# Who adds the residual, the weight sums and one low part: VectorE or transfers that accumulate, in the projection of a two-layer encoder trunk

## The chip, the core and the metric

The kernel runs on one core of a Trainium2 chip. A core has TensorE (PE, matrix products into PSUM), VectorE (DVE), ScalarE (ACT), GpSimd (POOL) and SyncE (SP), each of which runs its own list of instructions in order, and DMA engines that move data between HBM and the on-chip memory SBUF. Here SP issues nearly all loads and stores. POOL issues transfers that accumulate: they add what they carry to what lies at the destination. The metric is the device time of one launch in microseconds (us), the median of the runs.

## The reference

Two requests of 512 and 256 tokens (768 together) of width 1024 pass through two layers, all in fp32: layer 0 mixes tokens by windowed attention, layer 1 by a gated short convolution; each is followed by a squared-ReLU MLP of width 4096 and a gated input embedding.

```python
def short_conv(h, w_in, conv_w, w_out):
    b_gate, c_gate, u = jnp.split(h @ w_in, 3, axis=-1)
    z = c_gate * u
    ...                                   # conv: width 3 over tokens
    return (b_gate * conv) @ w_out

def trunk(x, p, ...):
    for i in range(DEPTH):                # 2
        h = rms_norm(x, norm_mix[i])
        x = x + (window_attention(h, ...) if i % 2 == 0 else short_conv(h, ...))
        h = rms_norm(x, norm_mlp[i])
        x = x + jnp.square(jax.nn.relu(h @ mlp_w_up[i])) @ mlp_w_down[i]
        gate = jax.nn.sigmoid(rms_norm(x, norm_ple[i]) @ ple_w_gate[i])
        x = x + (p[i] @ ple_w_proj[i]) * gate
    return rms_norm(x, final_norm)
```

The place of the change is the last line of `short_conv` in layer 1: the product with `w_out` (1024 x 1024), its addition to the residual `x`, and the start of the MLP behind it.

## The kernel before

**Stages.** By the trace, attention takes 0 to 285 us, the MLP of layer 0 to about 700, its gate and embedding to about 820, the product with `w_in` and the convolution to 1000 (12 chunks), the projection with `w_out` 1000 to 1067 (4 chunks), the MLP of layer 1 to about 1470, and the last gate, embedding and norm the rest.

**Products.** Activations lie with their features on the 128 partitions and tokens along the free axis, `x(0)` to `x(7)` being 128 x 768 tiles. A product of two blocks of weights with two blocks of activations is made with seven products in place of eight (a Strassen scheme; H = 384 is half of the tokens). Each needs a sum or difference of weight blocks (class `Weights7`) and of activation blocks. To keep fp32 accuracy, every operand is split: a high part, ACT's copy into the fp32r type (`whi`, `vhi`, `zhi`, line 922), and a low part, DVE's subtraction `src - hi` (`wlo`, `vlo`, `zlo`, line 933). PE computes high x high, high x low and low x high: 8 + 4 matmuls of 128 x 384 for each of the seven products (line 954). In some chunks, chunk 0 of the projection and the first of the MLP among them, a few are done apart with a smaller depth (line 966, `closing` and `parts`, whose operands stand at lines 866 to 879).

**A chunk** (`seven_parts`) handles a pair of weight tiles `r1`, `r2` (`wraw`, 128 x 1024, three places in SBUF). Its operands are four groups: `direct` (`whi`, `wlo`, from `r1`), `w22` (`vhi`, `vlo`, from half of `r2`), `s32` (`zhi`, `zlo`, from the sum tile `a`) and `s14` (`whi`, `wlo`, from the sum tile `b`). The sum tiles are called `sum`. They are made for the next chunk while the present one runs, on DVE: `sums32` makes `a` (lines 893, 894), `sums14` makes `b` (lines 901, 903), four operations of 128 x 512 in all. `zhi` and `zlo` have one place each, `whi` and `wlo` two. The order of the seven products on PE is `yh,whi`, then `t,zhi` into `b`, `t,zhi` into `a`, `yh,whi` into `c`, `t,whi` into `a`, `t,vhi` into `d`, `yh,whi` into `a`; each high half is followed by its low half. Behind the first product ACT copies `a` into `c` (line 2039), behind the second `b` into `p` (2046), behind the third `a` into `d` (2051); the products that follow need the copied places.

**Sums by transfers.** For the pairs named in `GATHERED` the sums are not made on DVE but by `gathered`: SP loads four halves of 256 KB into `a` and `b` (line 845), and POOL issues four accumulating transfers (line 847): 512 KB, 256, 256 and, from `a` into `b` within SBUF, 256 KB. In the projection these are chunk 1 and pair 4, which is the first chunk of the MLP (`first_up`). (Two more pairs elsewhere are gathered too; they stay.)

**The residual.** Before the projection, `x` has been stored into HBM as `xp` (line 2349). `Joined(c)` takes the products of chunk c into `x(c)` and `x(c + 4)`. For chunks in `BY_DMA` (0 and 1) it writes the product alone, two of the four quarters by ACT copies (lines 2763 and 2776), two by DVE (2755 and 2770), and afterwards POOL adds `xp` by two accumulating transfers of 384 KB (line 2936). For chunks 2 and 3 SP loads `xp` back into `x` first (line 2928) and DVE adds (lines 2758, 2759, 2765, 2772 and 2778). When `x(m)` is complete, `nxt.block` squares it for the next norm (`sq`, line 637) and `nxt.combine` makes the MLP's operands from it (`q`, `t`, `xs`).

**The order.** All of this is written once into a `Recorder`, which notes each operation with a cost in us and a delay until its result is there (`Recorder.add`), sets up a list schedule from them, and then issues the five engines' instructions in that order. So a cost or an operation that changes can move other operations too. The instructions of one engine stay in the order chosen, whatever really arrives first.

Of the kernel before, what the change touches and what calls it, by code (L numbers as in the profile page):

```python
# [17 lines left out]
AF = mybir.ActivationFunctionType  # L18
ALU = mybir.AluOpType
# [6 lines left out]
KB = D // P  # L26
# [7 lines left out]
CH = 1024  # L34
# [13 lines left out]
H = T // 2  # L48
# [68 lines left out]
def size(x):  # L117
    n = 1
    for m in x.shape[1:]:
        n *= m  # L120
    return n
# [26 lines left out]
class Recorder:  # L148
# [85 lines left out]
    def add(self, engine, what, run, outs, ins, line, table=None):  # L234
        n = max([1] + [size(ap) for ap in outs])
        if engine == "PE":
            cost = {384: 0.1735, 256: 0.121, 512: 0.23, 128: 0.11}.get(n, n * 0.45e-3)
            lag = cost + 0.16
        elif engine == "DVE":
            cost = 0.07 + n * 1.042e-3 + 0.06 * (what == "scalar_tensor_tensor" and n > 384)  # L240
            lag = cost + 0.082
        elif engine == "ACT" and what == "dma_start":
            cost, lag = 0.1, 4.0
        elif engine == "ACT":
            cost = 0.032 + n * 0.911e-3 + 0.09 * (len(ins) > 1)
            lag = cost + 0.095
            if table is not None:
                if table != self.tables[0]:
                    cost += 1.3
                    lag += 1.3  # L250
        elif engine == "SP":
            cost, lag = 0.46, 4 * P * n / 350e3
        elif what == "dma_start":
            cost, lag = 3.5, 5.0
        else:
            cost, lag = 0.3, 0.4
        op = Recorded(engine, run, cost, lag, line)
        op.size, op.due = n, self.due
        for ap in ins:
            self.touch(op, ap, False)  # L260
        for ap in outs:
            self.touch(op, ap, True)
        if self.also is not None:
            op.pre[self.also] = True
        if table is not None:
            if self.tables[1] is not None:
                op.pre.setdefault(self.tables[1], False)
            self.tables = table, op
        self.ops.append(op)
        return op  # L270
# [187 lines left out]
def trunk_kernel(ctx: ExitStack, tc: tile.TileContext, a: dict, out: bass.AP):  # L458
    nc = tc.nc
    record = Recorder(tc)  # L460
    act, dve, pe, sp, pool = (
        record.engine(*z)
        for z in ((nc.scalar, "ACT"), (nc.vector, "DVE"), (nc.tensor, "PE"), (nc.sync, "SP"), (nc.gpsimd, "POOL"))
    )
# [38 lines left out]
    def home(source, n, dt, tag, name, bufs=1):  # L503

        def make():
            return source.tile([P, n], dt, tag=tag, name=name, bufs=bufs)

        return make() if record.closed else record.new(tag, bufs, make, [P, n], dt)

    def fetch(src):  # L510
        raw = home(wp, CH, F32, "wraw", "wraw", 3)
        sp.dma_start(raw[:, : src.shape[1]], src)
        return raw
# [92 lines left out]
    class Norm:  # L606


        n = T

        def __init__(self, i, name, places, acc, rstd=None):
            self.i, self.name, self.places, self.rplace = i, name, places, rstd
            self.xs = [None] * KB, [None] * KB
            self.aplace, self.begun = acc, False
# [159 lines left out]
    class Sums:  # L774
# [20 lines left out]
        def high(self, i):  # L795
            t = [slot(self.places[2 * i + p], "t7") for p in range(2)]
            act.activation(t[0][:], (self.q1, self.q2)[i][:], AF.Copy)  # L797
            self.keep(t, (("t1", "t3"), ("t4", "t2"))[i])
            self.t = self.t + [t] if i else [t]
# [38 lines left out]
    def sum_places():  # L838
        return [home(more, CH, F32, f"sum{i}", "sum") for i in range(2)]

    def gathered(src1, src2):
        half, other = slice(0, 512), slice(512, CH)
        a, b = sum_places()
        for t, c, src in ((a, half, src1[:, half]), (a, other, src1[:, half]), (b, half, src2[:, half]), (b, other, src1[:, other])):
            sp.dma_start(t[:, c], src)
        for to, src in ((a[:], src2), (a[:, other], src2[:, half]), (b[:, half], src2[:, other]), (b[:, other], a[:, other])):
            pool.dma_start(to, src, accum_op=ALU.add)
        return a, b

    class Weights7:  # L850

        def __init__(self, src1, src2, sums=None):
            self.moved = sums is not None
            self.raw = [fetch(src1), fetch(src2)]
            self.w, self.parts, self.due, self.apart = {}, {}, set(), None
            self.s = sums or sum_places()
# [36 lines left out]

        def sums14(self, part=None):
            if self.moved:
                return
            (r1, r2), (a, b) = self.raw, self.s
            if part != 1:  # L900
                dve.tensor_tensor(b[:, :512], r2[:, :512], r2[:, 512:], ALU.add)
            if part != 0:
                dve.tensor_tensor(b[:, 512:], r1[:, 512:], a[:, 512:], ALU.add)

        def high(self, group):

            self.due.add(group)
            names = self.GROUPS[group]
            if group in ("s32", "s14"):
                src = self.s[group == "s14"][:]  # L910
            else:
                src = self.raw[group != "direct"][:, CH - 512 * len(names) :]
            n = len(names) * 512
            if group == "s32":
                tag = "z"
            else:
                tag = "v" if group == "w22" else None
            if tag is None:
                hi, lo = (home(wp, CH, F32R, f"w{p}", f"w{p}", 2) for p in ("hi", "lo"))
            else:  # L920
                hi, lo = (home(more, n, F32R, f"{tag}{p}", f"{tag}{p}") for p in ("hi", "lo"))
            act.activation(hi[:], src, AF.Copy)  # L922
            self.parts[group] = hi, lo, src
            for i, k in enumerate(names):
                c = slice(512 * i, 512 * i + 512)
                self.w[k] = hi[:, c], lo[:, c]
# [284 lines left out]
    def mixer_attention():  # L1211
# [109 lines left out]
        def split_op(hi, lo, src, n, ready, keys):  # L1321

            def high():
                act.activation(hi.t[:, :n], src()[:, :n], AF.Copy)

            def low():
                dve.tensor_tensor(lo.t[:, :n], src()[:, :n], hi.t[:, :n].bitcast(F32), ALU.subtract)

            h = first(hi, "ACT", A(n), high, ready, keys)
            return h, first(lo, "DVE", V(n), low, [h], [*keys, hi.key])  # L1330
# [597 lines left out]

    PAIRED = [m + i for m in range(KB // 2) for i in (0, KB // 2)]

    def up_chunk(l, u):
        f = 4 * (u // 2) + u % 2
        return Weights7(a["up"][l, f], a["up"][l, f + 2])


    def run(steps, n=None):
# [146 lines left out]
    def mlp(l, norm, nxt, w, places, early, spare, product=None, follow=None, closing=None):  # L2083
# [207 lines left out]
        with record.as_written({ET.Activation, ET.PE, ET.DVE}):  # L2291
            if product:
                ahead(norm, product, w, places[3:5] + places[6:7] + places[12:])
            for i, (job, *args) in enumerate(jobs):

                def make():

                    if i + 1 == len(jobs):
                        return None
                    what, *n = jobs[i + 1]  # L2300
                    if what is not down:
                        return up_chunk(l, *n)
                    k = (KB // 2) * n[0] + 2 * n[1]
                    return Weights7(a_down[k], a_down[k + 1])

                a_down = a["down"][l]
                w = job(*args, w, make, None)
            assert not pend
            return w
# [467 lines left out]
            else:  # L2777
                dve.tensor_tensor(self.one[:, H:], self.one[:, H:], a, ALU.add)

    GATHERED, BY_DMA = (1, 4), (0, 1)  # L2780

    def mixer_conv(norm, w, early, nxt, wide, held, yplaces, parts, closing=None, closing_out=None):

# [55 lines left out]
        class Out:  # L2839
            def __init__(self, kind):  # L2840
                self.kind = kind
# [38 lines left out]

        def out_weights(c):
            f = a["w_out"][c], a["w_out"][c + KB // 2]
            return Weights7(*f, sums=gathered(*f) if c in GATHERED else None)

        def first_up():
            f = a["up"][1, 0], a["up"][1, 2]
            return Weights7(*f, sums=gathered(*f) if KB // 2 in GATHERED else None)

        with record.as_written({ET.Activation, ET.PE, ET.DVE}):
            for n in range(3 * KB // 2):  # L2890
                j, kind = divmod(n, 3)
                bs = []
                last = n == 3 * KB // 2 - 1
# [58 lines left out]
    for i, m in enumerate(PAIRED):  # L2952
        if i == 1:
            w += [weight(a["w_o0"][3], 4)] * 2
        ps = both()
        if m < KB // 2:
            group2(ps, terms_of(w[m], [p[4:] for p in aos], col=m % 2 * P))
        else:
            group2(ps, terms_of(w2, [p[6:] for p in aos], col=(m - 4) * P))
        add(m, ps, xa[m])  # L2960
        n1.block(m, x(m))
        behind(i)
# [121 lines left out]
```

## Time and profile before

| what | us |
| --- | --- |
| median of 3 runs (1617.63, 1617.76, 1621.16) | 1617.76 |
| the profiled execution | 1618.11 |
| its span on the core | 1616.3 |
| PE busy, of the span | 1600.6 (99%) |
| DVE busy | 1410.8 (87%) |
| ACT busy | 978.9 (61%) |
| POOL busy (transfers it issues) | 117.4 (7%) |
| mean granted clock of PE | 0.997 |

The busy time of an engine counts its instructions, not the waits between them; the granted clock is the share of full speed that the chip let PE run at. In timelines a row is a start, a duration, the engine, the line of the kernel, output and inputs, and in brackets the time for which the engine was idle before it with what ended that idle time. `a<-t,zhi` means that `a` is written from `t` and `zhi`. The durations of neighbouring instructions overlap a little, as engines are pipelined. The 1.8 us between the span and the device time lie outside the core's instructions.

### The profile page before, as it was taken

The numbers are of one execution on the slowest core, as the hardware profiler recorded it, in microseconds if no ns is written. First come the engines' busy times: TensorE is split into PE (matmuls) and PEld (weight loads), VectorE is DVE, ScalarE is ACT, GpSimd is POOL, SyncE is SP. The second block draws the span as 40 slices with busy tenths as digits, with TensorE's granted clock in tenths as the row PEclk, the third lists the DMA queues.
The fourth block names the chain that finished last, engine by engine and source line by source line (L and its number), as shares of the span: only waits on it lengthen the run. The fifth ranks groups of instructions, "written<-read, shape, count | busy, mean of one in ns | idle before, by whom it ended". The sixth has DMA issues, their size and how long they took to land.

```text
span 1616.3 us, 24519 instructions
## 1 busy us (share of the span) xinstructions
PE 1600.6 (99%) x9217; PEld 1551.9 (96%) x9217; DVE 1410.8 (87%) x2300; ACT 978.9 (61%) x1574; POOL 117.4 (7%) x178
## 2 busy tenths in 40 slices
PE   9999999999999999999999999999999999999998
PEld 7988889999999999999999999899999999999987
DVE  7579997998888888999899988799988988889986
ACT  7378887765555555556684435576555545546655
POOL 1001000010110110100000000100110011010000
PEclk9999999999999999999999999999999999999999
DMA  8745314243433343315432213642443343342232
GB/s 298 214 122 150 111 37 131 105 114 83 117 108 93 100 104 94 103 66 153 139 107 91 73 71 86 182 111 78 119 105 93 103 114 87 87 118 78 85 122 88
DMA packets 68563, 179.45 MB, mean 111 GB/s; under 512 B 8379, under 2 KB 24123, under 8 KB 68444
## 3 DMA queue, kind: packets, MB, share of 16 engines
q1 hardware_dynamic: 51596, 152.06, 27.9%
q0 software_dynamic: 16704, 25.70, 9.8%
q8 instruction: 72, 1.18, 0.3%
q14 instruction: 47, 0.39, 0.1%
q10 hardware_dynamic: 144, 0.13, 0.0%
HBM read 135.39 MB, written 13.11 MB: 92 GB/s over the span
## 4 chain that ended last, share of the span: by engine, by line
PE 93%; ACT 3%; DVE 2%; DMA 1%; issue 1%; SPq 0%; POOL 0%; DVEq 0%; ACTq 0%; POOLq 0%
PE a L954 40%; PE b L954 10%; PE mm L436 8%; PE c L954 6%; PE d L954 6%; PE gate L558 4%; PE B L954 4%; PE C L954 4%; PE gate L2409 3%; PE O L436 2%; PE S L436 2%; PE pt L436 2%; PE vp L436 1%; PE mm L558 1%; DMA sum<-sum 0%
## 5 line engine op out<-in xcount | busy, mean ns | idle before, releaser
L933 DVE TENSOR_TENSOR zlo<-sum,zhi 128x1024 fp32r<-128x1024 f32 x80 | 97.7, 1221 | 61.1 <-ACT zhi L922 61.0
L922 ACT ACTIVATE whi<-sum 128x1024 fp32r<-128x1024 f32 x80 | 84.9, 1062 | 96.2 <-PE a L954 82.9
L922 ACT ACTIVATE vhi<-wraw 128x512 fp32r<-128x512 f32 x80 | 50.5, 631 | 140.9 <-PE B L954 62.5
L954 PE MATMUL a<-xs,whi 128*128 128x384 f32 x692 | 134.6, 334 | 0.0
L2241 POOL DMA_DIRECT2D x<-p x96 | 83.9, 874 | 681.5 <-issue 396.1
L954 PE MATMUL a<-t,zhi 128*128 128x384 f32 x610 | 126.9, 337 | 3.6 <-ACT c L2039 3.6
L954 PEld LDWEIGHTS a<-xs,whi 128*128 128x128 f32 x692 | 121.2, 188 | 0.2
L954 PE MATMUL a<-t,whi 128*128 128x384 f32 x562 | 116.1, 335 | 0.5 <-ACT d L2051 0.5
L954 PE MATMUL b<-t,zhi 128*128 128x384 f32 x562 | 116.3, 334 | 0.0
L954 PEld LDWEIGHTS a<-t,zhi 128*128 128x128 f32 x610 | 108.4, 189 | 4.5 <-ACT c L2039 4.5
L922 ACT ACTIVATE zhi<-sum 128x1024 fp32r<-128x1024 f32 x80 | 84.7, 1059 | 42.4 <-PE a L954 31.9
L954 PE MATMUL a<-act,whi 128*128 128x384 f32 x512 | 109.3, 334 | 0.0
L933 DVE TENSOR_TENSOR wlo<-sum,whi 128x1024 fp32r<-128x1024 f32 x80 | 97.4, 1218 | 5.0 <-ACT whi L922 5.0
L954 PEld LDWEIGHTS a<-t,whi 128*128 128x128 f32 x562 | 99.0, 188 | 1.4 <-ACT d L2051 1.3
L954 PEld LDWEIGHTS b<-t,zhi 128*128 128x128 f32 x562 | 99.0, 188 | 0.2
L922 ACT ACTIVATE whi<-wraw 128x1024 fp32r<-128x1024 f32 x80 | 84.3, 1054 | 23.3 <-PE C L954 17.2
L933 DVE TENSOR_TENSOR wlo<-wraw,whi 128x1024 fp32r<-128x1024 f32 x80 | 97.5, 1219 | 0.0
L954 PEld LDWEIGHTS a<-act,whi 128*128 128x128 f32 x512 | 90.6, 188 | 0.0
L436 PE MATMUL mm<-xs_mix,whi 128*128 128x512 f32 (+1 forms) x320 | 80.1, 340 | 0.0
L2202 DVE TENSOR_TENSOR x<-x,a 128x384 f32<-128x384 f32 x128 | 67.6, 548 | 9.9 <-PE a L954 9.9
L797 ACT ACTIVATE t<-y 128x768 fp32r<-128x768 f32 x64 | 53.7, 839 | 35.9 <-DVE y L793 22.8
L954 PE MATMUL a<-xs,wlo 128*128 128x384 f32 x346 | 74.1, 334 | 0.0
(431 smaller groups left out, 4331.5 us busy)
## 6 DMA issues: line engine op xcount, KB each, us to landing
wraw<-in_up SPq DMA_DIRECT2D x64, 512.0 KB, 3.5
wraw<-in_down SPq DMA_DIRECT2D x64, 512.0 KB, 3.4
x<-p POOLq DMA_DIRECT2D x96, 192.0 KB, 3.1
wraw<-in_w_in SPq DMA_DIRECT2D x24, 512.0 KB, 3.5
wraw<-in_gate SPq DMA_DIRECT2D x16, 512.0 KB, 3.5
wraw<-in_w_q SPq DMA_DIRECT2D x8, 512.0 KB, 4.7
wraw<-in_w_out SPq DMA_DIRECT2D x8, 512.0 KB, 3.5
x_in<-in_x SPq DMA_DIRECT2D x8, 384.0 KB, 7.7
```

The source lines that it names most:

```text
L436: return f(*args, **kw)
L558: pe.matmul(t, lhsT=w, rhs=x[:, o:e], start=first and i == 0 and j == 0, stop=last and i == n - 1 and j == 2)
L797: act.activation(t[0][:], (self.q1, self.q2)[i][:], AF.Copy)
L922: act.activation(hi[:], src, AF.Copy)
L933: dve.tensor_tensor(lo[:], src, hi[:].bitcast(F32), ALU.subtract)
L954: pe.matmul(ps, lhsT=a, rhs=b, start=start and i == 0, stop=i == len(terms) - 1, skip_group_check=True)
L2202: dve.tensor_tensor(t[:, o : o + H], t[:, o : o + H], f, op)
L2241: pool.dma_start(low[i][:, o : o + H], p[:, i * H : i * H + H], accum_op=ALU.add)
L2409: pe.matmul(ps.t[:, o : o + n], lhsT=a_, rhs=b_, start=begin and i == 0 and j == 0, stop=end and i == len(terms) - 1 and j == 2,)
```

## The change

The diff does three things, and changes one cost by which the order is found.

1. `BY_DMA` becomes empty. Chunks 0 and 1 are treated as 2 and 3 were: SP loads `xp` back into `x`, and DVE adds all quarters.
2. `GATHERED` becomes (0,), with a new function: `mostly_gathered` for chunk 0 loads three halves and issues three accumulating transfers; the fourth quarter of the sums (`b`'s second half) is one DVE addition (flag `last`). Chunk 1 and the first MLP chunk have their sums made on DVE again.
3. For the pairs 1 to 4 of `SENT` (5 is not used by any) and the second up chunk of the last MLP (`SENT_UP`), `zlo` is made in another way: ACT copies `-src` into `zlo` (line 936 after), and POOL adds `src` to it by an accumulating transfer of 512 KB within SBUF (line 937 after). DVE's subtraction is left out for this group.
4. The planner's cost of a POOL transfer of more than 384 elements per partition goes from (3.5, 5.0) to (5.0, 7.5): us on POOL's list, us until it has landed.

```diff
-            cost, lag = 3.5, 5.0
+            cost, lag = (5.0, 7.5) if n > H else (3.5, 5.0)
...
+    def mostly_gathered(src1, src2):
+        half, other = slice(0, 512), slice(512, CH)
+        a, b = sum_places()
+        for t, c, src in ((a, half, src1[:, half]), (a, other, src1[:, half]), (b, half, src2[:, half])):
+            sp.dma_start(t[:, c], src)
+        for to, src in ((a[:], src2), (a[:, other], src2[:, half]), (b[:, half], src2[:, other])):
+            pool.dma_start(to, src, accum_op=ALU.add)
+        return a, b
...
         def sums14(self, part=None):
             if self.moved:
+                if self.last and part != 0:
+                    dve.tensor_tensor(self.s[1][:, 512:], self.raw[0][:, 512:], self.s[0][:, 512:], ALU.add)
                 return
...
             act.activation(hi[:], src, AF.Copy)
+            if group == "s32" and self.sent:
+                act.activation(lo[:], src, AF.Copy, scale=-1.0)
+                pool.dma_start(lo[:], src, accum_op=ALU.add)
+                self.due.remove(group)
...
+    SENT_UP = ((1, 1),)
...
-        return Weights7(a["up"][l, f], a["up"][l, f + 2])
+        return Weights7(a["up"][l, f], a["up"][l, f + 2], sent=(l, u) in SENT_UP)
...
-    GATHERED, BY_DMA = (1, 4), (0, 1)
+    SENT = (1, 2, 3, 4, 5)
+    GATHERED, BY_DMA = (0, ), ()
...
-            return Weights7(*f, sums=gathered(*f) if c in GATHERED else None)
+            return Weights7(*f, sums=mostly_gathered(*f) if c in GATHERED else None, last=c in GATHERED, sent=c in SENT)
```

How this moves the instructions is seen best on three engines. First POOL, whose whole list in and around the projection is short. Before:

```order
L2793 MEMSET z 128x1 x6
L847 DMA sum<-in_w_out 128x1024
L847 DMA sum<-in_w_out 128x512 x2
L847 DMA sum<-sum 128x512
L2936 DMA x<-xp 128x768 x4
L847 DMA sum<-in_up 128x1024
L847 DMA sum<-in_up 128x512 x2
L847 DMA sum<-sum 128x512
L2241 DMA x<-p 128x384 x48
```

And after, with the lines of the new file:

```order
L2812 MEMSET z 128x1 x6
L856 DMA sum<-in_w_out 128x1024
L856 DMA sum<-in_w_out 128x512 x2
L937 DMA zlo<-sum 128x1024 x5
L2259 DMA x<-p 128x384 x48
```

Twelve transfers between the memsets of the convolution and the embedding's additions have become eight: the gather of chunk 0 with three, and five additions into `zlo`.

Next SP, the loads from the first weights of the projection (`in_w_out`) to the first ones of the MLP (`in_up`). Before:

```order
L512 DMA wraw<-in_w_out 128x1024 x3
L845 DMA sum<-in_w_out 128x512 x4
L512 DMA wraw<-in_w_out 128x1024 x3
L2928 DMA x<-xp 128x768 x4
L512 DMA wraw<-in_w_out 128x1024 x2
L512 DMA wraw<-in_up 128x1024
L845 DMA sum<-in_up 128x512 x2
```

And after:

```order
L512 DMA wraw<-in_w_out 128x1024
L854 DMA sum<-in_w_out 128x512 x2
L512 DMA wraw<-in_w_out 128x1024 x2
L854 DMA sum<-in_w_out 128x512
L2947 DMA x<-xp 128x768 x4
L512 DMA wraw<-in_w_out 128x1024 x3
L2947 DMA x<-xp 128x768 x4
L512 DMA wraw<-in_w_out 128x1024 x2
L512 DMA wraw<-in_up 128x1024 x6
```

Four loads of the residual now stand ahead of the fourth weight tile, which is the second one of chunk 1, and four more behind the sixth; the halves for the sums are three at chunk 0 and no more at chunk 1 and the MLP.

Last ACT, from the end of chunk 0 into chunk 1. Before:

```order
L2763 ACTIVATE x<-c 128x384
L871 ACTIVATE parts<-q 128x128
L2742 ACTIVATE t_10744<-ys 128x768
L2776 ACTIVATE x<-a 128x384
L2742 ACTIVATE t_10767<-ys 128x768
L922 ACTIVATE whi<-sum 128x1024
L922 ACTIVATE vhi<-wraw 128x512
L2039 ACTIVATE c<-a 128x384
L2046 ACTIVATE p<-b 128x384
```

And after:

```order
L936 ACTIVATE zlo<-sum 128x1024
L934 ACTIVATE whi<-wraw 128x1024
L2753 ACTIVATE yh<-ys 128x768
L934 ACTIVATE zhi<-sum 128x1024
L934 ACTIVATE vhi<-wraw 128x512
L2760 ACTIVATE t_10754<-ys 128x768
L934 ACTIVATE whi<-sum 128x1024
L2760 ACTIVATE t_10774<-ys 128x768
L749 ACTIVATE xs_10786<-x,vec 128x384
L2057 ACTIVATE c<-a 128x384
```

The two copies into `x` have gone to DVE, the negated copy into `zlo` has come, and `whi<-sum`, which stays ahead of the copy `c<-a`, now reads a sum that DVE makes.

More of the change, by code (lines that the diff above doesn't have):

```diff
@@ L848, in gathered, with __init__ @@
         return a, b
+    def mostly_gathered(src1, src2):
[6 more added lines that the diff above has]
+        return a, b
     class Weights7:
-        def __init__(self, src1, src2, sums=None):
-            self.moved = sums is not None
+        def __init__(self, src1, src2, sums=None, last=False, sent=False):
+            self.sent = sent
+            self.moved, self.last = sums is not None, last
             self.raw = [fetch(src1), fetch(src2)]
@@ L2882, in out_weights @@
             f = a["w_out"][c], a["w_out"][c + KB // 2]
-            return Weights7(*f, sums=gathered(*f) if c in GATHERED else None)
+            return Weights7(*f, sums=mostly_gathered(*f) if c in GATHERED else None, last=c in GATHERED, sent=c in SENT)
         def first_up():
             f = a["up"][1, 0], a["up"][1, 2]
-            return Weights7(*f, sums=gathered(*f) if KB // 2 in GATHERED else None)
+            return Weights7(*f, sums=mostly_gathered(*f) if KB // 2 in GATHERED else None, last=KB // 2 in GATHERED, sent=KB // 2 in SENT)
         with record.as_written({ET.Activation, ET.PE, ET.DVE}):
```

## The prediction

> **What bounds the kernel now.** The first view is the page's busy shares and the shares of the chain that ended last.
>
> ```profile
> span 1616.3 us, 24519 instructions
> PE 1600.6 (99%) x9217; PEld 1551.9 (96%) x9217; DVE 1410.8 (87%) x2300; ACT 978.9 (61%) x1574; POOL 117.4 (7%) x178
> PE 93%; ACT 3%; DVE 2%; DMA 1%; issue 1%; SPq 0%; POOL 0%; DVEq 0%; ACTq 0%; POOLq 0%
> ```
>
> TensorE is the bound, 99% busy, so an edit on the other engines pays only where it ends a wait of TensorE or a stretch at a lower clock; an edit that adds no such wait costs nothing. The diff touches the projection chunks and what is made there for the first MLP chunks, about 990 to 1090 us. So the second view is that stretch cut in windows of 20 us. Columns: window, sum of the window, then busy us and instructions of PE, weight loads, DVE, ACT and POOL, the granted clock, DMA share and GB/s.
>
> ```profile
> 990.00:1010.00 20.00, 20.00 (x117) 20.00 (x117) 19.82 (x30) 13.25 (x22) 2.64 (x3) 1.00 0.40 93
> 1010.00:1030.00 20.00, 16.86 (x82) 16.54 (x81) 12.07 (x19) 7.85 (x13) 2.63 (x3) 0.83 0.84 236
> 1030.00:1050.00 20.00, 19.74 (x110) 18.61 (x108) 18.82 (x27) 15.76 (x24) 1.75 (x2) 1.00 0.56 133
> 1050.00:1070.00 20.00, 19.47 (x113) 19.46 (x113) 20.00 (x30) 17.73 (x30) 3.52 (x4) 1.00 0.57 136
> 1070.00:1090.00 20.00, 19.13 (x109) 18.45 (x108) 18.84 (x30) 14.23 (x21) 0.00 (x0) 1.00 0.28 89
> ```
>
> An undisturbed window holds 117 matmuls, 20/117 = 0.171 us each. The four others hold 82 + 110 + 113 + 109 = 414 of 468. The 54 missing are 54 x 0.171 = 9.2 us, of which the window with the 0.83 clock has 35, 6.0 us. That is all there is to win here. Who makes PE wait between 1010 and 1090 us is the third view (us, times, longest), with the clock of the six us after the long wait below it:
>
> ```profile
> PE a L954 <- ACT c L2039: 3.1, 1, 3.1
> PE a L954 <- DVE x L2759: 0.5, 1, 0.5
> PE ss L677 <- ACT ah L499: 0.5, 1, 0.5
> PE a L966 <- DVE closing L867: 0.4, 1, 0.4
> ...
> 1023.00:1029.00 6.00, 6.00 (x19) 6.00 (x20) 3.34 (x6) 2.00 (x4) 0.87 (x1) 0.51 0.73 204
> ```
>
> One wait of 3.1 us, for ACT's copy `c` of a product in PSUM, is followed by a half clock: 19 matmuls in 6 us instead of 35, a further 2.7 us in this window. The fourth view, the timeline of ACT and POOL, says why that copy was late (start, us, engine, instruction, in brackets the idle time before it and its releaser):
>
> ```profile
> 1020.93 1.06 ACT L922 ACTIVATE whi<-sum 128x1024 fp32r<-128x1024 f32 x1 [4.04 <-DMA sum<-sum]
> 1022.41 0.47 ACT L2039 ACTIVATE c<-a 128x384 f32<-128x384 f32 x1
> ...
> 1012.81 0.87 POOL L847 DMA_DIRECT2D sum<-sum  x1 [3.34 <-issue]
> 1021.13 0.88 POOL L2936 DMA_DIRECT2D x<-xp  x1 [7.45 <-issue]
> ```
>
> ACT issues in order. `whi<-sum` of chunk 1 stands ahead of `c<-a` and waits 4.04 us for the last accumulating transfer of chunk 1's gather, so the 0.47 us copy on which PE depends starts at 1022.41. The transfer issued at 1012.81; the issues' view says how long such things take (KB each, median us to landing), first those issued from 1010 to 1021, then one load at 985, then 1050 to 1073:
>
> ```profile
> wraw<-in_w_out SPq DMA_DIRECT2D x3, 512.0 KB, 5.6
> x<-xp SPq DMA_DIRECT2D x4, 384.0 KB, 7.2
> sum<-sum POOLq DMA_DIRECT2D x1, 256.0 KB, 8.0
> ...
> wraw<-in_w_out SPq DMA_DIRECT2D x1, 512.0 KB, 3.4
> ...
> sum<-in_up POOLq DMA_DIRECT2D x1, 512.0 KB, 5.5
> sum<-in_up POOLq DMA_DIRECT2D x2, 256.0 KB, 4.9
> sum<-in_up SPq DMA_DIRECT2D x2, 256.0 KB, 4.2
> ...
> sum<-sum POOLq DMA_DIRECT2D x1, 256.0 KB, 3.3
> ```
>
> The same 256 KB addition that takes 3.3 us later took 8.0 beside three weight loads and four residual loads. That collision is the stall.
>
> **The change, part by part.** *Gathers of chunks 1 and 4.* Eight POOL additions go, and with them the wait of `whi<-sum`: the sums are again made by DVE. Chunk 0 is gathered instead, with three POOL additions and one DVE addition. *Residual.* POOL's four additions into `x` go; SP loads chunks 0 and 1 too, four more transfers of 384 KB, and DVE adds. *Low parts.* For chunks 1 to 3, the first up chunk and the second, ACT writes the negated sum into `zlo` and POOL adds the sum, so the subtraction on DVE goes. POOL's DMAs in the stretch: 4 + 4 + 4 before, 3 + 5 now. The prices on DVE and ACT:
>
> ```profile
> L933 DVE TENSOR_TENSOR zlo<-sum,zhi 128x1024 fp32r<-128x1024 f32 x7 | 8.5, 1218 | 4.0 <-ACT zhi L922 4.0
> L893 DVE TENSOR_TENSOR sum<-wraw 128x512 f32<-128x512 f32 x5 | 3.4, 684 | 0.0
> L2758 DVE TENSOR_TENSOR x<-x,p 128x768 f32<-128x768 f32 x2 | 1.9, 950 | 0.0
> L2759 DVE TENSOR_TENSOR x<-x,a 128x384 f32<-128x384 f32 x2 | 1.1, 547 | 0.0
> ...
> L922 ACT ACTIVATE zhi<-sum 128x1024 fp32r<-128x1024 f32 x7 | 7.3, 1049 | 0.9 <-PE a L954 0.9
> L2763 ACT ACTIVATE x<-c 128x384 f32<-128x384 f32 x2 | 1.0, 478 | 2.1 <-PE c L966 2.1
> L766 ACT ACTIVATE q<-x,vec 128x768 f32<-128x768 f32 x8 | 7.5, 932 | 8.0 <-DMA x<-xp 8.0
> L658 ACT ACT_TABLE_LOAD x1 | 1.3, 1283 | 0.0
> L499 ACT ACTIVATE ah<-acc_mlp 128x768 fp32r<-128x768 f32 x1 | 0.8, 822 | 0.0
> ```
>
> DVE: five subtractions go, -6.1 us; two chunks' sums return, 8 x 0.684 = +5.5; three of chunk 0's four go, -2.1; for each of two chunks one wide addition (0.95) and two narrow ones (2 x 0.547) come, +4.1, the other two narrow ones replacing two DVE operations of that size. Net +1.4 us, and +3.5 from 1010 us on, since chunk 0's sums lie earlier. ACT: five copies at the price of `zhi`, +5.2, four narrow copies away, -1.9; net +3.3. ACT was busy 55.6 of the 80 us and waited 8.0 for the residual's additions (row of `q`), which end, so its length is covered; what matters is its order.
>
> DVE's cover is thin. Its four windows add up to 69.7 us. If PE got all 9.2 us back, DVE would have 80 - 9.2 = 70.8 us for 69.7 + 1.4 = 71.1, at the 99% that 990 to 1010 shows (19.82 of 20) about 71.8: 1.0 us short. With all 3.5 after 1010 it is 73.2/0.99 = 73.9, 3.1 us short; with room ahead of 1010 and behind 1090 it can be none. I take 1.0, because DVE is full from 990 on and what chunk 0's sums save there moves later work forward; 0 and 3.1 stay as ends. Late next are therefore small waits of PE for DVE, such as the 0.5 us for `x` and 0.4 for `closing` above.
>
> *The new additions of `zlo`.* No SBUF-to-SBUF 512 KB addition is in the trace. The lower end is the undisturbed `sum<-sum` of 256 KB, 3.3 us, with 5.5 - 4.9 = 0.6 us for twice the bytes by the `in_up` rows: 3.9. The upper end is the crowded one, 8.0. I take 5.5, the 512 KB addition from HBM, since now one POOL DMA per chunk runs, not four in a row. `zlo` has one place, so ACT's copy follows PE's last reading in the chunk before:
>
> ```profile
> 1041.91 0.85 PE L954 MATMUL a<-t,zlo 128*128 128x384 f32 x4
> 1056.03 0.85 PE L954 MATMUL b<-t,zlo 128*128 128x384 f32 x4
> 1045.05 1.68 PE L954 MATMUL a<-t,whi 128*128 128x384 f32 x8 [0.20 <-ACT d L2051]
> 1007.67 0.68 PE L954 MATMUL a<-t,wlo 128*128 128x384 f32 x3
> ```
>
> A product is 8 high and 4 low matmuls, a chunk seven products. From the end of the third product's low half (`a<-t,zlo`) to the start of the next chunk's second low half (`b<-t,zlo`) PE has 84 + 20 - 36 = 68 matmuls, 11.6 us; the 13.3 us between the first two rows hold waits as well. ACT's copy takes 1.05 of them, and at four chunks it stands next to ACT's copy `d` of the third product, so it can start at once: 10.5 us are left for POOL's issue and landing. In the second up chunk it stands six rows behind `d`: `ah`, a table load, `whi`, `q` and two narrow `ln`, 0.8 + 1.3 + 1.05 + 0.9 + 2 x 0.5 = 5.1 us, and 5.4 are left. Against 5.5 that is even. I cost the additions at nothing; at 8.0 the one would be 2.6 us late. In front of `d` the copy also delays `d` by 1.05 us, in two chunks. The third row above is what that costs: there `zhi` stood ahead of `d`. So 0.2 each, and up to 1, within the 0 to 3.1.
>
> *SP's queue.* Eight loads of the residual now stand in it, and chunk 1's second weight load is queued behind the first four. The times come from two rows of DVE, the last subtraction before chunk 0's sum place is free and an operation of the last conv chunk:
>
> ```profile
> 978.16 1.23 DVE L933 TENSOR_TENSOR zlo<-sum,zhi 128x1024 fp32r<-128x1024 f32 x1 [2.75 <-ACT zhi L922]
> 1000.61 0.55 DVE L2854 TENSOR_TENSOR t<-d,p 128x384 f32<-128x384 f32 x1
> ```
>
> That load needs the place which DVE empties with its one addition into chunk 0's sum, and this now stands right behind `t<-d`. With 2.1 us less work before it: 1000.6 - 2.1 + 0.55 + 0.68 = 999.8 us. Landing in 3.4 us alone, or in 7.2 if as crowded as the four loads of before, it is there at 1003.2 or 1007.0. On DVE two additions of chunk 1 (2 x 0.684) wait for it and stand ahead of the `wlo` of chunk 0 (1.22 us), which PE reads at 1007.67 in the last of those four rows: ready at 1005.8 or at 1009.6, so 1.9 us early or 1.9 us late. I take the first, since the four loads wait only for PE's last readings of the conv stage and are issued some 4 us earlier. Chunk 0's gather has the place from 979.4 on: loads of 4.2, additions of 5.5 and 4.9 and a third of 4.9 to 8.0 give 994 for the sum that DVE's addition reads and 999 to 1002 for the one that feeds `wlo`, so it is hidden.
>
> *The planner's price* for wide POOL DMAs shifts rows elsewhere; there PE runs 117 matmuls in 20 us as from 990 to 1010, and I cost it at nothing, 0.5 us either way.
>
> Sum, against the profiled execution's 1618.11 us (span 1616.3): -9.2 + 1.0 = -8.2, so 1609.9. The median of the runs is 1617.76, 0.35 below it; by it 1609.5.
>
> **The rivals.** *B: chunk 0 waits for SP's queue.* The 1.9 us above come back as a wait of `a<-t,wlo` in chunk 0: 1609.5 + 1.9 = 1611.4. For it: four 384 KB loads ahead took 7.2 us. Against: the rest of POOL's and SP's traffic at that time is gone.
>
> *C: another long gap.* If a transfer is over 5 us late at one of these places, PE idles some 3 us and the clock falls again, as it did at 1020: about 6.0 us back, 1615.5, within the noise of the old time. Against: no wait in the stretch but that one exceeded 0.5 us, and B's worst is 1.9. The Trainium skill ("TensorE: Matmul & The Clock Gate", "HAM oscillation — how this bites in real kernels") puts the gap that halves the clock at more than about 3.4 us, the free-running window. The wait here was 3.1 and was followed by 0.51, so I would not count a gap of 3.0 safe; by the page's figure C would need a longer one and half its chance would go to B.
>
> *D: slower, the additions of `zlo` are late at every chunk.* POOL starts each after ACT's copy, and PE's second product of each chunk reads the result. From 5.4 us of issue and landing on one reaches PE, from 10.5 on all five. At 14 us they are 8.6 + 4 x 3.5 = 22.6 us late together: 1632. Against: POOL's rows from 1050 to 1063, while DVE was busy 20.00 of 20 us, landed in 4.9 and 5.5. The Trainium skill ("SBUF — State Buffer", "SBUF: two separate sides", the trap "DVE blocks DMA") has a rule that speaks against the change: while VectorE holds the shared port pair in a 2-port mode, the descriptors of a transfer from POOL's queue wait. The rows just named show no such delay, so it gets no more than D's chance.
>
> *E: the stall was something else* and only the small waits move: 1616 to 1618. Against: the chain from 1012.81 to 1022.93 is unbroken in the rows.
>
> **How the numbers follow.** A, stall gone and DVE up to 3.1 us short: 0.63, 1608.5 to 1611.6. B 0.17, to 1612.5. C 0.11, 1613 to 1617. D 0.06, above 1622.6. E 0.03. A measurement tells apart about 0.3%, 4.9 us, so faster means below 1612.9: A and B, 0.80. C and E are the same, 0.14; D is slower, 0.06. The predicted time is A's, 1609.5. The range goes from 1607.8 (no shortage, 0.5 us gained in the planner's order) to 1614.0, which leaves out most of C, D and E.
>
> **What would show it.** In the profile of the changed kernel: windows from 1010 to 1070 near 117 matmuls at clock 1.00; no wait of PE for `c` over 1 us; DVE at 99% and more there; the wait for `whi<-sum` gone from ACT; `zlo<-sum` landing in 4 to 8 us. I am wrong if a PE wait of 3 us or more with a lower clock stands anywhere from 995 to 1090 us, if PE waits for `zlo`, or if DVE's shortage stretches every chunk beyond 14.4 us (84 matmuls x 0.171).

## The result and the profile after

The changed kernel takes 1610.35 us (median of 6 runs, 1609.86 to 1610.88) beside 1617.75 us for the kernel before on the same chip: 7.4 us less, a ratio of 0.9952 with a 95% interval of 0.9939 to 0.9964. The profiled execution took 1609.86 us, its span went from 1616.3 to 1608.1, 8.2 us.

The page of the changed kernel, the same lines as before:

```profile
span 1608.1 us, 24512 instructions
PE 1597.0 (99%) x9217; PEld 1549.0 (96%) x9217; DVE 1411.5 (88%) x2306; ACT 982.5 (61%) x1575; POOL 114.3 (7%) x174
```

DVE's work grew by 0.7 us (1.4 expected; the durations in the sum overlap by some 0.08 us each), ACT's by 3.6 (3.3 expected). The stretch of the change, in the same windows:

```profile
990.00:1010.00 20.00, 20.00 (x116) 19.73 (x116) 19.30 (x29) 13.58 (x24) 2.43 (x3) 1.00 0.50 148
1010.00:1030.00 20.00, 19.69 (x113) 19.34 (x112) 20.00 (x35) 13.64 (x20) 0.89 (x1) 1.00 0.73 215
1030.00:1050.00 20.00, 20.00 (x117) 19.86 (x116) 19.96 (x31) 17.18 (x24) 0.87 (x1) 1.00 0.40 119
1050.00:1070.00 20.00, 20.00 (x116) 19.70 (x115) 20.00 (x30) 17.32 (x28) 0.88 (x1) 1.00 0.22 53
1070.00:1090.00 20.00, 20.00 (x116) 19.52 (x115) 19.96 (x33) 15.26 (x22) 0.87 (x1) 1.00 0.36 106
```

PE executes 113 + 117 + 116 + 116 = 462 matmuls from 1010 to 1090 us instead of 414, the clock is 1.00 throughout, and DVE is busy for 79.9 of the 80 us. The 48 matmuls that came back are 48 x 0.171 = 8.2 us, as much as the two profiled spans differ by. (A matmul across an edge counts in both windows; in one stretch of 80 us the counts are 409 and 456, 47 more.) The one wait of PE left from 990 to 1110 is this (us, times, longest):

```profile
PE a L982 <- DVE parts L2748: 0.3, 1, 0.3
```

Four of the five additions into `zlo` in this stretch (POOL's timeline), and the time from issue to landing of these four (windows that start at 1007, 1023, 1038 and 1072); the fifth, issued at 1053.50, landed in 4.6 us:

```profile
1007.79 0.88 POOL L937 DMA_DIRECT2D zlo<-sum  x1 [12.88 <-ACT zlo L936]
1024.08 0.89 POOL L937 DMA_DIRECT2D zlo<-sum  x1 [15.41 <-ACT d L2069]
1038.81 0.87 POOL L937 DMA_DIRECT2D zlo<-sum  x1 [13.85 <-ACT d L2069]
1072.20 0.87 POOL L937 DMA_DIRECT2D zlo<-sum  x1 [17.82 <-ACT zlo L936]
...
zlo<-sum POOLq DMA_DIRECT2D x1, 512.0 KB, 4.8
...
zlo<-sum POOLq DMA_DIRECT2D x1, 512.0 KB, 5.8
...
zlo<-sum POOLq DMA_DIRECT2D x1, 512.0 KB, 4.5
...
zlo<-sum POOLq DMA_DIRECT2D x1, 512.0 KB, 5.1
```

POOL now rests 13 to 18 us before each addition. Before, it issued most of its transfers 0.3 to 0.4 us after the one ahead had landed, such as the one at 1021.13 after 1012.81 + 8.0; the others waited for DVE or for a load. ACT no longer waits for any of POOL's transfers: `q` is held 0.8 us at most, by DVE, and so is one `whi<-sum`, 0.7 us at 1077.80. ACT's row of `q`:

```profile
1021.70 0.94 ACT L766 ACTIVATE q<-x,vec 128x768 f32<-128x768 f32 x1 [0.80 <-DVE x L2790]
```

### The profile page after: what moved, and what is told of

It is laid out like the page before. It is cut to its first block, busy times and chain, and to the rows that moved or that the text cites. A ratio compares the mean times of both kernels' runs of the same rounds, so it can differ in the third digit from the quotient of the medians.

```text
span 1608.1 us, 24512 instructions
## 1 busy us (share of the span) xinstructions
PE 1597.0 (99%) x9217; PEld 1549.0 (96%) x9217; DVE 1411.5 (88%) x2306; ACT 982.5 (61%) x1575; POOL 114.3 (7%) x174
## 4 chain that ended last, share of the span: by engine, by line
PE 94%; ACT 2%; DVE 2%; DMA 1%; issue 1%; SPq 0%; DVEq 0%; ACTq 0%
PE a L970 40%; PE b L970 10%; PE mm L436 8%; PE d L970 6%; PE c L970 6%; PE gate L558 4%; PE B L970 4%; PE C L970 4%; PE gate L2427 3%; PE O L436 2%; PE S L436 2%; PE pt L436 2%; PE vp L436 1%; PE mm L558 1%; PE a L982 1%
## 5 line engine op out<-in xcount | busy, mean ns | idle before, releaser
L949 DVE TENSOR_TENSOR zlo<-sum,zhi 128x1024 fp32r<-128x1024 f32 x75 | 91.7, 1222 | 57.7 <-ACT zhi L934 57.6
```

The costliest lines, as they stand in the source:

```text
L949: dve.tensor_tensor(lo[:], src, hi[:].bitcast(F32), ALU.subtract)
```

## The experiments

Ratios are against runs of the kernel before on the same chip. Most are of two kinds: parts of the change put into the kernel before, and parts taken out of the changed kernel. In all but the two that cut the additions of `zlo` the planner sets up its order anew, so some rows near the projection stand elsewhere, too.

**Chunk 1's gather alone taken away.**

```diff
-    GATHERED, BY_DMA = (1, 4), (0, 1)
+    GATHERED, BY_DMA = (4,), (0, 1)
```

> The kernel before, with one part of the change: chunk 1's sums are made by DVE, nothing else (GATHERED = (4,)). Theory (the 9.2 us were lost because ACT waited for the last addition of chunk 1's gather): its 6.0 us come back, less what four more DVE additions (2.7 us) cost where DVE is full: 1612.5, from 1611 to 1614, and no wait of PE for the copy c over 1 us. Rival 1 (the residual's transfers were what mattered, by ACT's 8.0 us of waits for x): no change, 1616 to 1618.

Measured: 1621.04 us beside 1618.73, ratio 1.0015 (1.0006 to 1.0024). Slower, outside what either theory gave. ACT's wait for the gather is gone, but PE has five others, four of them over 1 us. Three of these, then rows of ACT and DVE of this kernel:

```profile
1030.20 1.66 PE L954 MATMUL a<-yh,whi 128*128 128x384 f32 x8 [2.08 <-DVE x L2755]
1046.04 1.68 PE L954 MATMUL a<-t,whi 128*128 128x384 f32 x8 [2.42 <-ACT d L2051]
1073.19 2.29 PE L954 MATMUL a<-t,zhi 128*128 128x384 f32 x6 [2.78 <-ACT c L2039]
...
1025.80 0.94 ACT L766 ACTIVATE q<-x,vec 128x768 f32<-128x768 f32 x1 [3.42 <-DMA x<-xp]
1043.94 0.94 ACT L766 ACTIVATE q<-x,vec 128x768 f32<-128x768 f32 x1 [2.05 <-DMA x<-xp]
...
1026.77 0.56 DVE L787 TENSOR_TENSOR q<-q 128x384 f32<-128x384 f32 x1 [3.22 <-ACT q L766]
```

ACT waits 3.42 us for POOL's residual addition with `q`, and DVE, which needs `q`, idles 3.22 us behind it; its 2.7 us of returned sums come on top. At 1043.94 `q` waits 2.05 us again, the copy `d` stands behind it, and PE waits 2.42 us for `d`. So there was a second wait on ACT's list. How much of the loss is due to it, to the returned sums and to the new order was not tried apart.

**Only the fourth addition of that gather taken away.** The first three stay; the last SP half and the addition that took 8.0 us become one DVE addition, as in the changed kernel's `last`.

```diff
-            return Weights7(*f, sums=gathered(*f) if c in GATHERED else None)
+            return Weights7(*f, sums=gathered(*f, c == 1) if c in GATHERED else None, last=c == 1)
...
```

> The kernel before, with only the fourth of chunk 1's four POOL additions (the one that took 8.0 us) and the SP load under it replaced by one DVE addition. Theory: the third addition lands at about 1012.5, the stall is gone, 6 us come back: 1612, from 1611 to 1613.5. Rival 1: no change, 1616 to 1618. Rival 2 (any gather at chunk 1 is too late there, since the place of its sums is free too late): the wait moves to the third addition and most of the loss stays, 1615 to 1617.5.

Measured: 1615.95, ratio 0.9984 (0.9976 to 0.9993): 2.6 us of the 6.0. The time lies in the second rival's range, but not by its way: `whi<-sum` no longer waits for the gather, and the second wait stands bare. PE and ACT:

```profile
1026.53 2.51 PE L956 MATMUL a<-t,whi 128*128 128x384 f32 x8 [3.57 <-ACT d L2053]
...
1025.16 0.93 ACT L766 ACTIVATE q<-x,vec 128x768 f32<-128x768 f32 x1 [5.84 <-DMA x<-xp]
1026.00 0.47 ACT L2053 ACTIVATE d<-a 128x384 f32<-128x384 f32 x1
```

`q` waits 5.84 us for the residual's addition, `d` is queued behind it, and PE stands 3.57 us. In the kernel before, `q` waited 4.00 us at the same place, behind the first stall:

```profile
1027.28 0.93 ACT L766 ACTIVATE q<-x,vec 128x768 f32<-128x768 f32 x1 [4.00 <-DMA x<-xp]
```

This shows it: two of POOL's transfers held the same list, and the second takes over when the first is removed.

**The residual alone by SP and DVE.**

```diff
-    GATHERED, BY_DMA = (1, 4), (0, 1)
+    GATHERED, BY_DMA = (1, 4), ()
```

> The kernel before, with another part alone: the residual of chunks 0 and 1 loaded by SP and added by DVE (BY_DMA empty), the gathers of chunks 1 and 4 as before. Theory: the four loads now stand between the loads of chunk 1's halves, so its gather starts later and the stall stays or grows, and DVE has 4.1 us more to do: 1618 to 1622. Rival 1 (the residual's transfers were what mattered): 1610 to 1613.

Measured: 1625.82, ratio 1.0042 (1.0029 to 1.0055), more than the theory's range. The gather does not start later, as expected (998.04 us, before 998.16), but beside the new loads its first addition took 8.6 us to land instead of 5.6 and its third 7.8 instead of 3.9. So the fourth is issued at 1019.55 instead of 1012.81, and the same chain is longer:

```profile
1029.99 2.61 PE L954 MATMUL a<-t,zhi 128*128 128x384 f32 x7 [10.00 <-ACT c L2039]
...
1025.93 1.06 ACT L922 ACTIVATE whi<-sum 128x1024 fp32r<-128x1024 f32 x1 [11.93 <-DMA sum<-sum]
...
1019.55 0.87 POOL L847 DMA_DIRECT2D sum<-sum  x1 [7.27 <-issue]
```

**These two parts together**, in the kernel before.

```diff
-    GATHERED, BY_DMA = (1, 4), (0, 1)
+    GATHERED, BY_DMA = (4,), ()
```

> The kernel before with two parts of the change at once: chunk 1's sums by DVE and the residual loaded by SP (GATHERED = (4,), BY_DMA empty); nothing is sent by negated copies, chunk 0 is not gathered. Each part alone came out slower than before (+2.3 and +7.1 us). Theory of two waits (on ACT's list the wait for the gather stands in front of a second one, q for POOL's residual addition; either alone holds ACT's copies c and d, and each part removes one and makes the other later): together they gain, 1613.5 to 1617 beside 1618.7 for the kernel before. Rival (the parts cost DVE more than they bring, only the sent low parts make the gain): the losses add up, 1622 to 1628.

Measured: 1616.86 beside 1617.50, ratio 0.9993 (0.9985 to 1.0002). The single losses (+2.3 and +7.1) did not add up, which speaks against the rival: together they are level with the kernel before, and no long gap is left. The gain of 1.7 us or more that the theory of two waits gave did not come either. What remains are three waits of PE for `c`, 1.7 us at most, and others of 0.5 us or less. In the window of the first, DVE is full; ahead of the longest, at 1067.94, ACT waits for the gather of the first MLP chunk, which this kernel keeps, and DVE idles 2.17 us behind ACT. What that gather costs by itself was not tried. A window, PE's waits for `c` from 985 to 1130, and ACT's wait:

```profile
1030.00:1050.00 20.00, 19.04 (x110) 18.72 (x109) 20.00 (x30) 14.56 (x20) 0.88 (x1) 1.00 0.30 104
PE a L954 <- ACT c L2039: 3.9, 3, 1.7
...
1060.72 1.06 ACT L922 ACTIVATE zhi<-sum 128x1024 fp32r<-128x1024 f32 x1 [2.56 <-DMA sum<-in_up]
```

**The third part alone**: the five negated copies and additions into `zlo` (chunks 1 to 3, first and second up chunk) in the kernel before.

```diff
             act.activation(hi[:], src, AF.Copy)
+            if group == "s32" and self.sent:
+                act.activation(lo[:], src, AF.Copy, scale=-1.0)
+                pool.dma_start(lo[:], src, accum_op=ALU.add)
+                self.due.remove(group)
...
```

> The kernel before with the third part alone: the five zlo by negated copies and POOL additions; gathers of chunks 1 and 4 and the residual's additions as before. Theory of POOL's queue (every transfer of POOL waits for the one ahead; 4 + 4 + 4 + 5 = 17 of about 5 us stand in 90 us): the residual's additions and the sums land later still, ACT waits for them with c and d behind it, 1620 to 1630. Rival (the 6.1 us that DVE is spared are the gain): 1611 to 1614.

Measured: 1637.83, ratio 1.0124 (1.0110 to 1.0138). The direction is the theory's, the size is not: it priced ACT's waits, but PE also waits for `zlo` itself, 7.98 us in the row below and 4.12 at 1085.21.

```profile
1019.34 0.89 POOL L925 DMA_DIRECT2D zlo<-sum  x1 [2.72 <-issue]
1028.42 0.88 POOL L2940 DMA_DIRECT2D x<-xp  x1 [8.20 <-issue]
...
1028.15 1.65 PE L958 MATMUL b<-t,zlo 128*128 128x384 f32 x4 [7.98 <-DMA zlo<-sum]
```

With 17 transfers on POOL's queue an addition of `zlo` took 8.8 us from 1019.34 on, and everything behind it moved back. The part that makes the change's gain complete costs 20 us where the queue is not empty.

**The changed kernel without it** (all low parts by DVE).

```diff
-    SENT = (1, 2, 3, 4, 5)
+    SENT = ()
-    SENT_UP = ((1, 1),)
+    SENT_UP = ()
```

> The changed kernel with all low parts made by DVE (SENT and SENT_UP empty). Theory (DVE is the next bound behind the stall: it is 99.8% busy from 1010 to 1110 us in the changed kernel): 6.1 us more on DVE stretch PE by 3 to 6 us, 1613.5 to 1616.5, as many waits of PE for DVE below 1 us each. Rival 3 (DVE's queue has room before 1000 and behind 1110, the sent low parts bring nothing): 1610 to 1611.5.

Measured: 1615.26, ratio 0.9977 (0.9968 to 0.9986), against 0.9952 with it: 0.0025 x 1618 = 4.0 us, an estimate, for the five subtractions (6.1 us of DVE). DVE is full and PE's windows have holes, waits for ACT's `c` and `d` of 1.5 us at most. ACT waits for DVE in turn, though some of the lateness may be its own new order. Two windows, and the longest of ACT's waits for DVE in them:

```profile
1030.00:1050.00 20.00, 18.96 (x109) 18.64 (x109) 20.00 (x30) 14.84 (x20) 0.00 (x0) 1.00 0.22 70
1050.00:1070.00 20.00, 18.00 (x99) 16.45 (x98) 19.96 (x28) 16.77 (x27) 0.00 (x0) 1.00 0.14 45
...
1046.28 0.94 ACT L766 ACTIVATE q<-x,vec 128x768 f32<-128x768 f32 x1 [2.00 <-DVE x L2790]
```

**The changed kernel without chunk 0's gather.**

```diff
-    GATHERED, BY_DMA = (0, ), ()
+    GATHERED, BY_DMA = (), ()
```

> The changed kernel with chunk 0's sums by DVE too (GATHERED empty): 2.1 us more on DVE at 985 to 1000, no gather on POOL. Theory (DVE is full from 990 to 1110, what is added ahead of it is pushed through): 1.0 to 2.5 us more, 1611.5 to 1613.5. Rival (room ahead of 990, where DVE was 15 of 20 us busy, takes it up): 1610 to 1611.

Measured: 1612.32, ratio 0.9967 (0.9954 to 0.9979): 2.0 us above the changed kernel's median (2.4 by the ratios) for 2.1 us of DVE work. So what is put ahead of the full stretch passes through it, about one to one, though DVE was only 15.33 of 20 us busy from 970 to 990.

**The changed kernel with the residual added by POOL.**

```diff
-    GATHERED, BY_DMA = (0, ), ()
+    GATHERED, BY_DMA = (0, ), (0, 1)
```

> The changed kernel with the residual of chunks 0 and 1 added by POOL again (BY_DMA = (0, 1)), all else as changed. Theory of two waits: ACT's q waits for x<-xp with c or d behind it, PE waits 2 to 4 us there as in the run that only took the gather away, and POOL's additions also delay those into zlo: 1614 to 1620. Rival (without chunk 1's gather the residual's additions land in time, and DVE has 4.1 us less to do): 1610 to 1611.5.

Measured: 1617.68, ratio 1.0003 (0.9995 to 1.0012). The time is in the theory's range, the way is another: `q` waits only 0.69 us in this order. DVE idles first and is overrun afterwards.

```profile
1010.00:1030.00 20.00, 20.00 (x116) 19.73 (x115) 14.01 (x21) 11.98 (x17) 2.18 (x3) 1.00 0.81 235
1030.00:1050.00 20.00, 18.88 (x106) 18.01 (x105) 17.04 (x27) 16.03 (x24) 3.09 (x4) 1.00 0.71 153
1050.00:1070.00 20.00, 16.46 (x89) 15.21 (x89) 20.00 (x32) 18.17 (x28) 0.87 (x1) 0.97 0.22 53
```

DVE is busy 14.0 and 17.0 of 20 us, then 20.0, while PE drops to 89 matmuls. Whether DVE's idle time comes from the residual stays open: its first long idle, 2.11 us at 1021.19, stands ahead of an addition of weight tiles and has no releaser in the profile, the next, 2.78 us at 1026.60, is for ACT's `whi`. That putting this one part back takes the whole gain away is shown.

**How much room the additions of `zlo` have**, by cutting each into pieces that POOL issues one after the other; every engine's order stays that of the changed kernel.

```diff
+    if "pieces" in kw:
+        to, src = (real(z) for z in args)
+        m = to.shape[1] // kw["pieces"]
+        for i in range(kw["pieces"]):
+            done = f(to[:, m * i : m * i + m], src[:, m * i : m * i + m], accum_op=kw["accum_op"])
+        return done
...
-                pool.dma_start(lo[:], src, accum_op=ALU.add)
+                pool.dma_start(lo[:], src, accum_op=ALU.add, pieces=4)
```

The second kernel has `pieces=2`.

> The changed kernel, each 512 KB addition into zlo cut into four of 128 KB, one after the other on POOL; every engine's order as in the changed kernel. From rows of the changed kernel an addition takes 4.5 to 5.8 us and PE reads 6.9, 4.1, 5.4, 4.3 and 2.3 us after its landing. Four pieces at 3.3 to 3.8 us each are 13 to 15 us, some 9.5 later. Theory (PE waits for what exceeds the room): 2.6 + 5.4 + 4.1 + 5.2 + 7.2 = 24.5 us later, more with the half clock behind each gap over 3 us: 1635 to 1652. Rival (pieces run side by side on POOL's queue and land within the room): 1610 to 1613.

Measured: 1642.00, ratio 1.0155 (1.0141 to 1.0168).

> As the run with four pieces, but two of 256 KB, about 8.5 us instead of 5, 3.5 later. Theory: only the second up chunk (2.3 us of room) and, by ACT's copy for the products done apart, the first up chunk (3.0) are late, 0.5 to 1.7 us together, no half clock: 1611.5 to 1613.5 beside 1611 for the changed kernel. Rival (every addition is on the path): over 1618.

Measured: 1613.10, ratio 0.9972 (0.9961 to 0.9982). The time is in the range given, but it is about 3 us above the changed kernel, where 0.5 to 1.7 were expected. With four pieces the sum comes out, but not where it was expected. DVE's and PE's timelines, four pieces first, then DVE's with two:

```profile
1025.84 0.69 DVE L915 TENSOR_TENSOR sum<-wraw 128x512 f32<-128x512 f32 x1 [8.67 <-DMA zlo<-sum]
...
1027.45 0.69 PE L982 MATMUL b<-t,zhi 128*128 128x384 f32 x1 [7.52 <-DVE t L815]
...
1050.32 0.69 DVE L915 TENSOR_TENSOR sum<-wraw 128x512 f32<-128x512 f32 x1 [0.77 <-DMA zlo<-sum]
```

DVE's first addition for the next chunk (line 903 in the changed kernel) overwrites the sum that POOL's addition still reads, and there is one place for it. DVE waits 8.67 us, `t` is queued behind, and PE waits for `t`. The first to need an addition is thus DVE and not PE at chunks 1 to 3. At the second up chunk it is PE, which waits 2.33 us for `zlo` with four pieces. In the changed kernel these are the rows, DVE's at the three chunks and PE's at the second up chunk:

```profile
1016.57 0.69 DVE L903 TENSOR_TENSOR sum<-wraw 128x512 f32<-128x512 f32 x1
1031.55 0.69 DVE L903 TENSOR_TENSOR sum<-wraw 128x512 f32<-128x512 f32 x1
1047.02 0.68 DVE L903 TENSOR_TENSOR sum<-wraw 128x512 f32<-128x512 f32 x1
1079.57 0.85 PE L970 MATMUL b<-t,zlo 128*128 128x384 f32 x4
```

With the issues and landings shown above, the room behind the landing is 16.6 - 12.6 = 4.0 us at chunk 1, 31.6 - 29.9 = 1.7 at chunk 2, 47.0 - 43.3 = 3.7 at chunk 3 and 79.6 - 77.3 = 2.3 at the second up chunk; at the first up chunk it is 3.0, to ACT's copy of a part of `zlo` at 1061.13. By the estimate made for this run two pieces need some 3.5 us more, which is too much at chunk 2 and about even at chunk 3. PE's named waits with two pieces add up to 1.7 us, so a part of the 3 us stays open.

**The changed kernel with the planner's old cost.**

```diff
-            cost, lag = (5.0, 7.5) if n > H else (3.5, 5.0)
+            cost, lag = 3.5, 5.0
```

> The changed kernel with the planner's old cost of POOL's transfers (3.5, 5.0): same operations, in the projection other places for some 50 to 130 rows on each engine. Theory (the cost moves rows but opens no wait, as the prediction had it at 0 to 0.5): 1610 to 1612. Rival (the planner then reads zlo and the sums earlier than they land, 4.5 to 5.8 us against 5.0, and DVE or PE waits): 1612 to 1616.

Measured: 1609.86, ratio 0.9952 (0.9938 to 0.9966), the same as the changed kernel. The new cost moves rows and brings nothing beyond the interval, 2.3 us to either side.

## Why the prediction was right, and where its steps were not

The forecast was 1609.5 us, the result is 1610.35, inside the range and the way that was said. Case A held: every window has its clock of 1.00, no wait for `c`, DVE at 99.9%.

- *9.2 us to win.* Right as a sum: 54 missing matmuls before, 6 after, 8.2 us returned as forecast. (The bottom of the range has a slip: 1609.5 - 1.0 - 0.5 is 1608.0, not 1607.8.)
- *Whose stall it was.* Incomplete. The prediction gave 6.0 us to chunk 1's gather alone and counted ACT's 8.0 us for the residual only as cover that becomes free. The gather taken away alone made the kernel slower, without its fourth addition 2.6 us faster: a second wait, `q` for POOL's residual addition, stood behind the first on ACT's list. Had the change been the gather's removal alone, the same reasoning would have forecast the wrong sign, as it did for that run (1612.5 expected, 1621.04 measured). The change removes both waits, so the step did no harm here; that is luck. Why the fourth addition took 8.0 us, which the prediction put down to the seven loads beside it, was not tried apart.
- *DVE short by 1.0 us, ends 0 and 3.1.* Right as a size: 6 matmuls, 1.0 us, are still missing, 4 of them in the first window, though PE's one named wait for DVE is 0.3 us. That DVE is the next bound is borne out by two runs: 6.1 us more on it cost 4.0, 2.1 us more cost 2.0. Without chunk 0's gather and the sent low parts (the two other parts together, with the gather of the first MLP chunk kept) the gain is within the noise.
- *Additions of `zlo` at 5.5 us, ends 3.9 and 8.0.* They took 4.5 to 5.8. Their room, counted from the end of ACT's copy, was given as 10.5 us at four chunks and 5.4 at the second up chunk. It is 9.2, 7.9 and 8.6 at chunks 1 to 3, where the DVE operation that overwrites the source comes before PE's reading, and 8.0 at the first up chunk, to ACT's copy; only PE's reading had been counted. At the second up chunk it is 7.8, since PE reads 14.9 us after it has done with the chunk before, and not 11.6. Behind the landing 1.7 to 4.0 us are left, least at chunk 2, so the cost of nothing held, but by a margin that the prediction did not know.
- *SP's queue (rival B).* The second weight load of chunk 1 took 5.2 us, between the 3.4 and 7.2 assumed. DVE waited 0.7 us for it, and `wlo` of chunk 0 was ready at 1006.14 + 1.22 = 1007.36, just when PE read it, at 1007.42, instead of 1.9 us before. That B's wait stayed away is a near miss:

```profile
1004.60 0.69 DVE L903 TENSOR_TENSOR sum<-wraw 128x512 f32<-128x512 f32 x1 [0.70 <-DMA wraw<-in_w_out]
1006.14 1.22 DVE L949 TENSOR_TENSOR wlo<-sum,whi 128x1024 fp32r<-128x1024 f32 x1
...
1007.42 0.79 PE L970 MATMUL a<-t,wlo 128*128 128x384 f32 x3
```

- *Rival C* was priced about right: in the kernel without the fourth addition a gap of 3.57 us is followed by a granted clock of 0.58 over the next 3.5 us, and 1010 to 1050 us lack 36 matmuls, 6.2 us beside C's 6.0. *Rival D* is real but far: it takes additions of about 13 to 17 us (four pieces, 1642) or a queue of 17 transfers (1637.8). Beside a DVE that is 99.9% busy POOL's additions landed in 4.5 to 5.8 us, and no delay shows. The trap that the Trainium skill describes in "SBUF — State Buffer" ("SBUF: two separate sides", "DVE blocks DMA") is not seen with these operations of DVE; no run here shows whether any of them is in the 2-port mode that it names, so this is no test of it.
- *The planner's cost at nothing*: shown, within the 2.3 us of that run's interval.

## What to carry to other kernels

When an engine that issues in order waits for a transfer, look at what its next instructions wait for before counting the first wait as the gain: the next one may come from the same queue. Here two parts that each lose, 2.3 and 7.1 us, are level together; the gain came with the change's other parts. A transfer that takes over an engine's work has two ends: count the room up to whoever overwrites its source, too, and to every reader. And moving work to a queue paid here when the queue had been emptied first; the same five additions brought 4.0 us on POOL's emptied queue and cost 20 on the full one.

## What the runs showed of the hardware

How short a gap halves PE's clock was not expected. Rows of PE behind a gap, and windows of 4 us, in the kernel with the sent parts alone, in the changed kernel with POOL's residual, and, windows alone, in the kernel without chunk 1's gather:

```profile
1064.89 2.65 PE L958 MATMUL a<-t,zhi 128*128 128x384 f32 x8 [1.76 <-ACT c L2043]
1064.00:1068.00 4.00, 3.11 (x11) 3.11 (x12) 4.00 (x7) 2.43 (x5) 0.85 (x1) 0.66 0.58 131
...
1067.97 0.79 PE L970 MATMUL a<-xs,whi 128*128 128x384 f32 x3 [2.14 <-DVE xs L750]
1068.00:1072.00 4.00, 3.73 (x13) 3.22 (x14) 4.00 (x6) 3.54 (x7) 0.00 (x0) 0.61 0.36 131
...
1044.00:1048.00 4.00, 1.97 (x11) 1.97 (x12) 3.09 (x5) 4.00 (x6) 0.00 (x0) 1.00 0.12 32
1048.00:1052.00 4.00, 4.00 (x25) 4.00 (x24) 3.96 (x7) 1.66 (x4) 0.81 (x1) 1.00 0.39 123
```

Gaps of 1.76 and 2.14 us were followed by 0.66 and 0.61, while the gap of 2.42 us that ends at 1046.04 left the clock at 1.00 in its own window and in the next. So length alone does not decide; what else does, such as where the gap falls, was not tried. The Trainium skill ("TensorE: Matmul & The Clock Gate", "HAM oscillation — how this bites in real kernels") gives about 3.4 us for the gap that lowers the clock; by the rows above about half of that can be enough.
